# A two-block transformer kernel on one core: input norm reordered, rotations joined in pairs, norm boundaries and last quarter rearranged, two up projections 512 wide

## The chip, the cores and the metric

The kernel runs on one core of one Trainium2 chip. The metric is the device time of one execution in microseconds (us), as the median of several runs. The engines are named as in the profile: PE is TensorE's matmul side and PEld its weight loads, DVE is VectorE, ACT is ScalarE, POOL is GpSimd, and SP is SyncE, whose queue issues most DMAs.

## What is computed

The input has 256 tokens of width 1024. A first block puts 16 meta tokens in front and computes a convolution branch and a sparse attention branch, merged by gates, then an FFN with a short convolution. A second block of four steps follows (gated linear attention, FFN, block attention, FFN), each with a residual and a layer norm. All of it is fp32.

```python
h = rms_norm(stream, mix_norm_g[l])                 # stream: 16 meta tokens + x
u_conv, q, k, v, q_idx, k_idx, w_idx, gates = jnp.split(h @ w_in[l], split_at, axis=-1)
q = rope(q.reshape(bsz, seq_len, N_HEADS, HEAD_DIM), pos)
k = rope(k.reshape(bsz, seq_len, N_KV_HEADS, HEAD_DIM), pos)
q_idx = rope(...); k_idx = rope(...)
y_a = conformer_conv_branch(...)  # a*sigmoid(gate), 31-tap depthwise conv, layer norm, silu, @ pw_out
y_b = dsa_sparse_attention(...)   # keys chosen by index scores, softmax, @ w_o
g_a, g_b = jnp.split(jax.nn.sigmoid(gates), 2, axis=-1)
stream = stream + (g_a * y_a + g_b * y_b) @ w_merge_out[l]
h = rms_norm(stream, ffn_norm_g[l])
up = causal_depthwise_conv(h @ ffn_up[l], ffn_dw_w[l], ffn_dw_b[l])
a, b_ = jnp.split(up, 2, axis=-1)
stream = stream + (jax.nn.silu(a) * b_) @ ffn_down[l]
...
# second block, for the GLA mixer and then the MoBA mixer:
#   x = layer_norm_2(ALPHA * x + mixer(x));  x = layer_norm_2(ALPHA * x + swiglu_ffn(x))
# swiglu_ffn: gate, up = split(x @ w_gu); (silu(gate) * up) @ w_down
```

## The kernel before, in words

**Matmuls.** Every operand is split into a high and a low fp32r part, and a product is three matmuls: high by high, high by low, low by high. `mm_ws` (L175 to L177) keeps the weights stationary and streams the activations, transposed as hT, oT and so on (256 to 272 wide). `mm_xs` (L181 to L183) keeps the activations stationary and streams 512 columns of weights. Eight k steps of such triples make one projection tile (`proj_tile`). There are four PSUM buffers named ps_acc and four named ps_wk, each 512 wide.

**Weights.** They stream from DRAM in chunks of 2048 columns on SP's queue (wraw, three buffers). ACT makes the high part of a half chunk (whi, L134) and DVE the low one (wlo, L136), five halves ahead.

**The first block.** The input norm (from L283 on) transposes the raw x on PE, gets the row factors rw by `rsqrt` and `spread`, and forms hT in its two parts on ACT (L333) and DVE (L344). Then come the convolution's input (hp), keys, index heads, gates, eight query heads and the attention. `rope` rotates a head: two ACT copies swap the halves into sw, DVE multiplies by the tables twice and adds. Index scores are L474 and L477, softmax is L534 to L538, attention output oT has its low part made at L202.

**The convolution** of 31 taps is background work. Most taps are multiply-adds on DVE (L389, into yc). Some products are made on ACT (L406): one kind goes to a tile z with two buffers of its own tag, and DVE adds it to yc (L412); the other kind goes to zs, and a POOL DMA adds it into ysum, which DVE adds to yc at the end (L423). After that the layer norm of the convolution runs at high priority (L645 to L654 on DVE and PE's L648), and its result sT is needed for the projection by pw_out. While it runs, PE does the eight output projections of the attention (L175 to L177 from oT); DVE's L664 takes each out of its ps_acc buffer.

**Order.** A scheduler turns the program order into one queue for each engine: what is written earlier has priority, and each engine then works its queue strictly in order. At the norm boundaries and at the input norm the order is written out by hand: the strings in `ORDER` for the four layer norms name steps of `LayerNorm` (capital letters for the first 128 rows, small ones for the second: A add, S stats, G rsqrt, C center, F finish, L low part; g, x, t, k for other steps). `to_T` (L245) transposes a normed tile for the next projection.

**FFNs 2 and 3** (the SwiGLU ones): up projections in ps_wk, `evac2` (L936, L937) makes silu(a)·b, `split` its two parts rg_h and rg_l (L200, L202), and `mm_xs` the down projection into four ps_acc quarters, in groups of two hidden tiles; a ring keeps the last tiles of the FFN for the end. Then `norms` and the output.

Of the kernel before, what the change touches and what calls it, by code (L numbers as in the profile page):

```python
# [59 lines left out]
WARM = 9  # L60
FIRST = []
for _k in range(KT + 1):
# [22 lines left out]
def tile_hybrid(ctx: ExitStack, tc: tile.TileContext, x, meta, wts, misc, vec, cst, rows, gkw, ng, pos,  # L85
# [93 lines left out]
    def mm_xs(ps, xk, w, first, last):  # L179
        (wh, wl), (xh, xl) = w, xk  # L180
        PE.matmul(ps, xh, wh, start=first, stop=False)  # L181
        PE.matmul(ps, xh, wl, start=False, stop=False)  # L182
        PE.matmul(ps, xl, wh, start=False, stop=last)  # L183
# [38 lines left out]
    hT = (per.tile([P, KT, L], F32R, name="hT_h"), per.tile([P, KT, L], F32R, name="hT_l"))  # L222
# [18 lines left out]
    def to_T(src, xT, t, g, defer=False):  # L241
        pt = ps_wk().rearrange("p (a b) -> p a b", a=4)
        for a in range(4):
            k = 4 * g + a
            PE.transpose(pt[:, a, :], src[:, k * P:(k + 1) * P], ident)  # L245
# [35 lines left out]
    pj = ps_acc()  # L281
    for _ in range(WARM):
        PE.matmul(pj[:, :P], ones, ones, start=True, stop=True)  # L283
# [13 lines left out]
    with tc.high_priority(), tc.manual_schedule(engines={ENG.PE, ENG.DVE, ENG.Activation}):  # L297
        for k in range(KT):
            PE.transpose(pm[:, k * META:(k + 1) * META], mt[:, k * P:(k + 1) * P], ident[:META, :META])
        turn(0)  # L300
# [9 lines left out]
        A.activation(rw[:, :META], pr[:, :META], AF.Copy)  # L310
# [5 lines left out]
        for t in range(2):  # L316
            spread(rs[:, t:t + 1], META + t * P, P)
# [107 lines left out]
    def rope(o, ps, a, b, ti, parts=()):  # L425
        n = b - a
        sw = sc.tile([P, L], F32, name="sw", tag="s1", bufs=2)[:, :n]
        t1 = sc.tile([P, L], F32, name="t1", tag="s2", bufs=3)[:, :n]
# [21 lines left out]
    qi = []  # L450
    qi4 = mp.tile([P, 4, SEQ], F32, name="qi", tag="qi")
    for j in range(4):
        pq = ps_acc()
        proj_tile(pq[:, :SEQ], hT, META, L)
        q_ = qi4[:, j, :]
        rope(q_, pq[:, :SEQ], META, L, 2)
        qi.append(q_)
# [62 lines left out]
    qT = mp.tile([P, KT, NQ], F32, name="qT", tag="qT")  # L520
    for h in range(N_HEADS):
        pq = ps_acc()
        proj_tile(pq[:, :NQ], hT, T0, L)
        rope(qT[:, h, :], pq[:, :NQ], T0, L, 0)
# [6 lines left out]
    def soft(ps, b, n):  # L531
        l_ = sc.tile([P, L], F32, name="l_", tag="s2", bufs=3)[:, :n]
# [177 lines left out]
    def ffn(xT, n, pd, first, evac, ring, begun=None, then=None):  # L710
        f = 0
        while f < NF:
# [5 lines left out]
            for j in range(f, f + g):  # L718
# [4 lines left out]
                proj_tile(pa[:, :n], xT, 0, n, late=j == 0)  # L723
                proj_tile(pb[:, :n], xT, 0, n, late=j == 0)
# [38 lines left out]

    pd = [[ps_acc(), ps_acc()] for _ in range(2)]
# [7 lines left out]
    with tc.high_priority(), tc.manual_schedule(engines={ENG.DVE, ENG.Activation}):  # L772
        for t in range(2):
# [8 lines left out]
            for nn in range(2):  # L782
                s = slice(nn * 512, (nn + 1) * 512)
                V.scalar_tensor_tensor(x_[:, s], pd[t][nn], r, fg[:, s], op0=OP.mult, op1=OP.mult)
                lo.append(to_T(x_, hT, t, nn, defer=True))
# [9 lines left out]
    HV = [slice(nn * 512, (nn + 1) * 512) for nn in range(2)]  # L795

    class LayerNorm:
        def __init__(self, t, gi):
# [3 lines left out]
            self.bs = sc.tile([P, 2, 6], F32, name="bs", tag="bs", bufs=2)  # L802

        def add(self, nn):
# [3 lines left out]
        def stats(self, nn):  # L808
            V.bn_stats(self.bs[:, nn, :], self.y[:, HV[nn]])
# [11 lines left out]
        def finish(self, nn):  # L821
            s = HV[nn]
# [73 lines left out]
    def xs_late(ps, ws, t):  # L896
# [5 lines left out]
        for k, (wh, wl), c in at:  # L902
            PE.matmul(ps, hT[1][:, k, sl], wh[:, c], start=False, stop=k == KT - 1)  # L903

    def ffn_first(ring):
# [6 lines left out]
        def act(t):  # L912
            ps = first.ps[t]
            g_ = sc.tile([P, SEQ], F32, name="g_", tag="s2", bufs=3)
# [19 lines left out]
    def evac2(f, pa, pb):  # L934
        g_ = sc.tile([P, SEQ], F32, name="g_", tag="s2", bufs=3)
        A.activation(g_, pa[:, :SEQ], AF.Silu)  # L936
        V.tensor_mul(g_, g_, pb[:, :SEQ])  # L937
# [254 lines left out]
    ffn(hT, SEQ, pd, True, evac2, ring, begun)  # L1192
# [126 lines left out]
```

## Time and profile before

| what | us |
|---|---|
| runs | 1075.49, 1076.04, 1076.05 |
| median | 1076.04 |
| the profiled execution's own time | 1076.28 |
| its span, first to last instruction | 1074.5 |
| PE busy | 1054.8 (98%) |
| PEld busy | 954.5 (89%) |
| DVE busy | 739.5 (69%) |
| ACT busy | 601.0 (56%) |
| POOL busy | 44.1 (4%) |

All numbers taken from the trace are against the span. A matmul's duration in the trace holds a modelled end, so the cost of one is read from start to start, not from its duration. A row of the timeline is start, length, engine, line, operation, output and inputs, shapes, the number of instructions joined in it, and in brackets how long the engine was idle before it and what ended that.

### The profile page before, as it was taken

What the parts mean: (1) busy time and instruction counts of PE and PEld (TensorE: products, weight loads), DVE (VectorE), ACT (ScalarE), POOL (GpSimd) and SP (SyncE); (2) the same over time, 40 slices, a digit from 0 to 9 for tenths busy, and PEclk for the clock granted to TensorE, in tenths of its full rate; (3) what the DMA queues carried; (4) which work ended last, traced back from release to release, by engine and by line L of the source; (5) the groups of instructions that cost most, each with busy time, mean ns of one, the idle gap of its engine ahead of it and who ended that gap; (6) DMA issues with size and microseconds to landing.
All of it is one profiled execution on the core that took longest, in us unless ns stands there. A gap on an engine that the chain in (4) does not pass through costs nothing. (4 is left out here: it accounts for less than half of the span.)

```text
span 1074.5 us, 17515 instructions
## 1 busy us (share of the span) xinstructions
PE 1054.8 (98%) x6989; PEld 954.5 (89%) x6989; DVE 739.5 (69%) x1291; ACT 601.0 (56%) x1051; POOL 44.1 (4%) x52
## 2 busy tenths in 40 slices
PE   8999999999999999999999999999999999999997
PEld 8998998899899999977877999999888878999995
DVE  6899999995776767774577655556674766555555
ACT  6897698564555555567463444446256925444440
POOL 0131002100000000000000000000000000000000
PEclk8999999999999999999999999999999999999999
DMA  8886556564354555454453655557263436555541
GB/s 307 246 201 161 191 166 178 148 220 169 142 197 160 195 182 192 174 185 139 153 202 112 236 196 179 180 191 274 79 215 138 164 131 226 187 195 194 173 144 40
DMA packets 33333, 192.37 MB, mean 179 GB/s; under 512 B 3889, under 2 KB 7857, under 8 KB 12002
## 3 DMA queue, kind: packets, MB, share of 16 engines
q1 hardware_dynamic: 28002, 185.02, 49.7%
q0 software_dynamic: 5248, 6.23, 3.6%
q8 instruction: 55, 0.90, 0.3%
q14 instruction: 28, 0.23, 0.1%
HBM read 183.96 MB, written 1.05 MB: 172 GB/s over the span
## 5 line engine op out<-in xcount | busy, mean ns | idle before, releaser
L136 DVE TENSOR_TENSOR wlo<-wraw,whi 128x1024 fp32r<-128x1024 f32 x320 | 388.5, 1223 | 204.8 <-ACT whi L134 203.9
L134 ACT ACTIVATE whi<-wraw 128x1024 fp32r<-128x1024 f32 x322 | 337.3, 1058 | 302.0 <-PE ps_wk L176 117.7
L176 PE MATMUL ps_wk<-hT_l,whi 128*128 128x256 f32 (+1 forms) x976 | 274.9, 282 | 0.0
L177 PE MATMUL ps_wk<-hT_h,wlo 128*128 128x256 f32 (+1 forms) x976 | 274.6, 281 | 0.0
L175 PE MATMUL ps_wk<-hT_h,whi 128*128 128x256 f32 (+1 forms) x976 | 274.2, 281 | 0.0
L175 PEld LDWEIGHTS ps_wk<-hT_h,whi 128*128 128x128 f32 x976 | 184.4, 189 | 1.1
L176 PEld LDWEIGHTS ps_wk<-hT_l,whi 128*128 128x128 f32 x976 | 184.0, 189 | 1.4
L177 PEld LDWEIGHTS ps_wk<-hT_h,wlo 128*128 128x128 f32 x976 | 184.8, 189 | 0.4
L181 PE MATMUL ps_acc<-whi,rg_h 128*128 128x512 f32 x328 | 131.1, 400 | 0.0
L182 PE MATMUL ps_acc<-wlo,rg_h 128*128 128x512 f32 x328 | 129.6, 395 | 0.0
L183 PE MATMUL ps_acc<-whi,rg_l 128*128 128x512 f32 x328 | 127.1, 395 | 0.0
L175 PE MATMUL ps_acc<-hT_h,whi 128*128 128x258 f32 (+2 forms) x352 | 101.9, 290 | 0.0
L177 PE MATMUL ps_acc<-hT_h,wlo 128*128 128x258 f32 (+2 forms) x352 | 100.7, 286 | 0.0
L176 PE MATMUL ps_acc<-hT_l,whi 128*128 128x258 f32 (+2 forms) x352 | 100.5, 285 | 0.0
L183 PEld LDWEIGHTS ps_acc<-whi,rg_l 128*128 128x128 f32 x328 | 61.6, 188 | 14.7 <-DVE rg_l L202 0.2
L181 PEld LDWEIGHTS ps_acc<-whi,rg_h 128*128 128x128 f32 x328 | 61.6, 188 | 14.1 <-ACT rg_h L200 0.2
L182 PEld LDWEIGHTS ps_acc<-wlo,rg_h 128*128 128x128 f32 x328 | 61.7, 188 | 12.8
L181 PE MATMUL ps_acc<-whi,hT_h 128*128 128x512 f32 (+1 forms) x184 | 71.8, 390 | 0.0
L183 PE MATMUL ps_acc<-whi,hT_l 128*128 128x512 f32 (+1 forms) x184 | 70.8, 385 | 0.0
L182 PE MATMUL ps_acc<-wlo,hT_h 128*128 128x512 f32 (+1 forms) x184 | 70.6, 384 | 0.0
L175 PEld LDWEIGHTS ps_acc<-hT_h,whi 128*128 128x128 f32 x352 | 66.2, 188 | 0.3
L176 PEld LDWEIGHTS ps_acc<-hT_l,whi 128*128 128x128 f32 x352 | 66.3, 188 | 0.2
(950 smaller groups left out, 1561.7 us busy)
## 6 DMA issues: line engine op xcount, KB each, us to landing
wraw<-in_wts_dram SPq DMA_DIRECT2D x166, 1024.0 KB, 5.0
ysum<-zs POOLq DMA_DIRECT2D x10, 258.0 KB, 6.9
x<-in_x_dram SPq DMA_DIRECT2D x4, 512.0 KB, 3.8
lg<-in_rows_dram SPq DMA_DIRECT2D x4, 512.0 KB, 3.6
lb<-in_rows_dram SPq DMA_DIRECT2D x4, 512.0 KB, 5.4
wraw<-in_wts_dram SPq DMA_DIRECT2D x2, 512.0 KB, 6.5
out_dram<-x SPq DMA_DIRECT2D x4, 256.0 KB, 2.0
mraw<-in_misc_dram SPq DMA_DIRECT2D x1, 576.0 KB, 12.3
```

What stands on the lines that cost most here:

```text
L134: A.activation(hi, r, AF.Copy)
L136: V.tensor_sub(lo, r, hi.bitcast(F32))
L175: PE.matmul(ps, wh, xh, start=first, stop=False)
L176: PE.matmul(ps, wh, xl, start=False, stop=False)
L177: PE.matmul(ps, wl, xh, start=False, stop=last)
L181: PE.matmul(ps, xh, wh, start=first, stop=False)
L182: PE.matmul(ps, xh, wl, start=False, stop=False)
L183: PE.matmul(ps, xl, wh, start=False, stop=last)
```

## The change

1. **Input norm.** The first x tile is transposed after the meta tokens' row factor is spread; the two copies of rw go from ACT to DVE; the spread of the x rows' factors comes after the meta part of hT; five warm products on PE follow it.
2. **Rotations.** `rope_two` rotates two index heads (both in one ps_acc) or two query heads (the first six) in joined instructions. The swapped halves are in a tile sw2 with the tag z, that is in the two buffers of the convolution's z.
3. **Buffers.** Tag s2 (t1, l_, g_) has four buffers instead of three.
4. **Up projections of FFNs 2 and 3.** `proj_pair` streams the high and the low part of hT, which are now one tile, in one 512-wide matmul against the high weights, then the high part alone against the low weights. `evac2` adds the two halves of the result.
5. **Norm boundaries.** Manual dependencies (`BEHIND`) put the first transposes of each tile behind a certain matmul at the end of the first block; x and g change places in the first string of `ORDER`.
6. **Last quarter.** In the last FFN the last six hidden tiles of the last quarter go to two 256-wide ps_wk tiles; the last layer norm takes them in two pieces, with the sum of the residual and the rest (p1) ahead.

```diff
-WARM = 9
+WARM = (9, 5)
+BEHIND = (3, 2)
 ORDER = (
-    "A0 S0 A1 S1 G C0 C1 a0 F0 F1 s0 a1 L0 s1 L1 g x c0 c1 f0 f1 l0 l1 k x",
+    "A0 S0 A1 S1 G C0 C1 a0 F0 F1 s0 a1 L0 s1 L1 x g c0 c1 f0 f1 l0 l1 k x",
...
-    "A0 S0 A1 S1 G C0 C1 F0 F1 a0 s0 a1 s1 g c0 c1 f0 f1",
+    "p1 A0 S0 A1 S1 G C0 C1 F0 F1 a0 s0 a1 s1 a2 s2 g c0 c1 f0 f1 f2",
+    def proj_pair(ps):
+        w = next_half()
+        both = ps.rearrange("p (a b) -> p a b", a=2)
+        for k in range(KT):
+            wh, wl = cols(w, k * P, (k + 1) * P)
+            PE.matmul(both, wh, hT2[:, :, k, :SEQ], start=k == 0, stop=False)
+            PE.matmul(ps[:, :SEQ], wl, hT2[:, 0, k, :SEQ], start=False, stop=k == KT - 1)
...
-        turn(0)
...
-        A.activation(rw[:, :META], pr[:, :META], AF.Copy)
+        V.tensor_copy(rw[:, :META], pr[:, :META])
+        turn(0)
         turn(1)
...
-        for t in range(2):
-            spread(rs[:, t:t + 1], META + t * P, P)
...
+        for t in range(2):
+            spread(rs[:, t:t + 1], META + t * P, P)
+        for _ in range(WARM[1]):
+            PE.matmul(pz[:, :P], ones, ones, start=True, stop=True)
         later = []
-        A.activation(rw[:, META:], pr[:, META:], AF.Copy)
         emit_split(1, later)
+        V.tensor_copy(rw[:, META:], pr[:, META:])
...
+    def rope_two(o, ps, a, b, ti):
+        n = b - a
+        two = lambda i: tabs[:, i:i + 1, a:b].to_broadcast([P, 2, n])
+        sw = mp.tile([P, 2, NQ], F32, name="sw2", tag="z", bufs=2)[:, :, :n]
+        if len(ps) == 1:
+            both = ps[0].rearrange("p (a b) -> p a b", a=2)
+            A.activation(sw[0:64], both[64:128], AF.Copy)
+            A.activation(sw[64:128], both[0:64], AF.Copy)
+            V.tensor_mul(o, both, two(ti))
+        else:
+            for i, p in enumerate(ps):
+                A.activation(sw[0:64, i, :], p[64:128], AF.Copy)
+                A.activation(sw[64:128, i, :], p[0:64], AF.Copy)
+                V.tensor_mul(o[:, i, :], p, tabs[:, ti, a:b])
+        V.tensor_mul(sw, sw, two(ti + 1))
+        V.tensor_add(o, o, sw)
...
     for h in range(N_HEADS):
-        pq = ps_acc()
-        proj_tile(pq[:, :NQ], hT, T0, L)
-        rope(qT[:, h, :], pq[:, :NQ], T0, L, 0)
+        pqs.append(ps_acc()[:, :NQ])
+        proj_tile(pqs[-1], hT, T0, L)
+        if h >= N_HEADS - 2:
+            rope(qT[:, h, :], pqs[-1], T0, L, 0)
+        elif h % 2 == 1:
+            rope_two(qT[:, h - 1:h + 1, :], pqs[-2:], T0, L, 0)
...
+            if f + g == NF and ends:
+                order = order[:-g]
...
+            if f + g == NF and ends:
+                for a in range(0, 512, 256):
+                    ps = ps_wk()[:, :256]
+                    for i in range(g):
+                        mm_xs(ps, (acts[i][0][:, P:], acts[i][1][:, P:]), cols(ws[i], 512 + a, 768 + a),
+                              i == 0, i == g - 1)
+                    lasts.append(ps)
...
     def evac2(f, pa, pb):
-        g_ = sc.tile([P, SEQ], F32, name="g_", tag="s2", bufs=3)
-        A.activation(g_, pa[:, :SEQ], AF.Silu)
-        V.tensor_mul(g_, g_, pb[:, :SEQ])
+        g_, u_ = (sc.tile([P, SEQ], F32, name="g_", tag="s2", bufs=4) for _ in range(2))
+        A.activation(g_, pa[:, SEQ:], AF.Copy)
+        V.tensor_add(g_, g_, pa[:, :SEQ])
+        A.activation(g_, g_, AF.Silu)
+        A.activation(u_, pb[:, SEQ:], AF.Copy)
+        V.tensor_add(u_, u_, pb[:, :SEQ])
+        V.tensor_mul(g_, g_, u_)
         return g_
```

In the rows that follow the number behind a name tells tiles of one name apart. Lines are those of the changed kernel where rows are of the changed kernel: L406 there is L389 before (taps), L429 is L412 (z adds), L440 is L423 (final adds), L702 is L664, L686 is L648, L211 is L202, L137 is L136, L209 is L200, L1011 to L1016 are `evac2`.

DVE at the end of the convolution, before: the two splits of the last attention output, and the first output projection's gate product L664.

```order
L202 TENSOR_TENSOR oT_l_1518<-ps_wk_2286,oT_h_1517 128x4x128
L389 SCALAR_TENSOR_TENSOR yc_734<-hp_240,dwh_239,yc_734 128x243 x4
L389 SCALAR_TENSOR_TENSOR yc_734<-hp_240,dwh_239,yc_734 128x242
L202 TENSOR_TENSOR oT_l_1518<-ps_wk_2291,oT_h_1517 128x4x128
L389 SCALAR_TENSOR_TENSOR yc_734<-hp_240,dwh_239,yc_734 128x242
L423 TENSOR_TENSOR yc_734<-yc_734,ysum_2297 128x1032 x2
L136 TENSOR_TENSOR wlo_2698<-wraw_2101,whi_2697 128x1024
L645 TENSOR_TENSOR sqb_2618<-yc_734 128x516 x2
L664 SCALAR_TENSOR_TENSOR tg1_1520<-tg1_1520,ps_acc_2696 128x258
```

The same place after, from the second split on:

```order
L211 TENSOR_TENSOR oT_l_1490<-ps_wk_2263,oT_h_1489 128x4x128
L406 SCALAR_TENSOR_TENSOR yc_739<-hp_245,dwh_244,yc_739 128x258 x3
L429 TENSOR_TENSOR yc_739<-yc_739,z_2508 128x2x257
L406 SCALAR_TENSOR_TENSOR yc_739<-hp_245,dwh_244,yc_739 128x257 x2
L406 SCALAR_TENSOR_TENSOR yc_739<-hp_245,dwh_244,yc_739 128x256 x2
L406 SCALAR_TENSOR_TENSOR yc_739<-hp_245,dwh_244,yc_739 128x255 x4
L406 SCALAR_TENSOR_TENSOR yc_739<-hp_245,dwh_244,yc_739 128x254 x2
L406 SCALAR_TENSOR_TENSOR yc_739<-hp_245,dwh_244,yc_739 128x253 x2
L429 TENSOR_TENSOR yc_739<-yc_739,z_2530 128x2x253
L406 SCALAR_TENSOR_TENSOR yc_739<-hp_245,dwh_244,yc_739 128x252 x4
```

And after, the end of that run:

```order
L429 TENSOR_TENSOR yc_739<-yc_739,z_2568 128x2x245
L406 SCALAR_TENSOR_TENSOR yc_739<-hp_245,dwh_244,yc_739 128x245 x2
L406 SCALAR_TENSOR_TENSOR yc_739<-hp_245,dwh_244,yc_739 128x244 x2
L406 SCALAR_TENSOR_TENSOR yc_739<-hp_245,dwh_244,yc_739 128x243 x4
L406 SCALAR_TENSOR_TENSOR yc_739<-hp_245,dwh_244,yc_739 128x242 x2
L137 TENSOR_TENSOR wlo_2670<-wraw_2073,whi_2669 128x1024
L440 TENSOR_TENSOR yc_739<-yc_739,ysum_2269 128x1032
L702 SCALAR_TENSOR_TENSOR tg1_1492<-tg1_1492,ps_acc_2668 128x258
```

Where one tap stood behind the last split, 45 taps and five z adds stand there now (the rows between the two pieces go on in the same way).

PE at the convolution's layer norm, before: output projection 3 is in ps_acc_2790, and the sum over channels L648 stands ten matmuls into it.

```order
L175 MATMUL ps_acc_2790<-oT_h_1517,whi_2187 128x258
L176 MATMUL ps_acc_2790<-oT_l_1518,whi_2187 128x258
L177 MATMUL ps_acc_2790<-oT_h_1517,wlo_2188 128x258
L175 MATMUL ps_acc_2790<-oT_h_1517,whi_2187 128x258
L648 MATMUL ps_wk_2619<-sqb_2618,ones_77 128x258 x2
```

After, the last rows ahead of the same sum (L686):

```order
L176 MATMUL ps_acc_2792<-oT_h_1489,whi_2201 128x258
L177 MATMUL ps_acc_2792<-oT_l_1490,whi_2201 128x258
L178 MATMUL ps_acc_2792<-oT_h_1489,wlo_2202 128x258
L176 MATMUL ps_acc_2792<-oT_h_1489,whi_2201 128x258
L686 MATMUL ps_wk_2591<-sqb_2590,ones_77 128x258 x2
```

The sum has moved from output projection 3 to 13 matmuls into output projection 4 (ps_acc_2792), which is the fifth to ask for one of the four ps_acc buffers.

ACT in a group of FFN 2, before (L936 is the silu, L200 makes rg_h):

```order
L134 ACTIVATE whi_6852<-wraw_6762 128x1024
L936 ACTIVATE g__6880<-ps_wk_6820 128x256
L134 ACTIVATE whi_6887<-wraw_6762 128x1024
L200 ACTIVATE rg_h_6453<-g__6880 128x256
L134 ACTIVATE whi_6917<-wraw_6826 128x1024
```

After:

```order
L135 ACTIVATE whi_6794<-wraw_6712 128x1024
L1011 ACTIVATE g__6814<-ps_wk_6770 128x256
L1013 ACTIVATE g__6814<-g__6814 128x256
L1014 ACTIVATE g__6815<-ps_wk_6771 128x256
L135 ACTIVATE whi_6826<-wraw_6712 128x1024
L209 ACTIVATE rg_h_6425<-g__6814 128x256
```

Two copies out of PSUM are new, the second of them after the group's last up projection and ahead of a weight split.

More of the change, by code (lines that the diff above doesn't have):

```diff
@@ L182, in mm_xs @@
         PE.matmul(ps, xh, wl, start=False, stop=False)
-        PE.matmul(ps, xl, wh, start=False, stop=last)
+        return PE.matmul(ps, xl, wh, start=False, stop=last)
     def cols(w, a, b):
@@ L221, in tile_hybrid @@
     V.memset(ones, 1.0 / D)
-    hT = (per.tile([P, KT, L], F32R, name="hT_h"), per.tile([P, KT, L], F32R, name="hT_l"))
+    hT2 = per.tile([P, 2, KT, L], F32R, name="hT")
+    hT = (hT2[:, 0], hT2[:, 1])
     gl = [per.tile([P, KT, 16], F32R, name=f"gl{i}") for i in range(2)]
@@ L239, in row_bcast, with behind, to_T @@
         return t
-    def to_T(src, xT, t, g, defer=False):
+    def behind(turned, mark):
+        tc.add_manual_dep(turned.ins, mark.ins.name, LATER, reason="order")
+    def to_T(src, xT, t, g, defer=False, turned=None):
         pt = ps_wk().rearrange("p (a b) -> p a b", a=4)
@@ L279, in tile_hybrid @@
     nc.sync.dma_start(mraw, misc.rearrange("p (a b) -> p a b", a=KT))
-    pj = ps_acc()
-    for _ in range(WARM):
+    pj, pz = ps_acc(), ps_acc()
+    for _ in range(WARM[0]):
         PE.matmul(pj[:, :P], ones, ones, start=True, stop=True)
@@ L708, in tile_hybrid, with ffn @@
         go_on()
-    def ffn(xT, n, pd, first, evac, ring, begun=None, then=None):
+    def ffn(xT, n, pd, first, evac, ring, begun=None, then=None, ends=False):
         f = 0
@@ L722, in ffn @@
                 pa, pb = ps_wk(), ps_wk()
-                proj_tile(pa[:, :n], xT, 0, n, late=j == 0)
-                proj_tile(pb[:, :n], xT, 0, n, late=j == 0)
+                for ps in (pa, pb):
+                    if begun:
+                        proj_pair(ps)
+                    else:
+                        proj_tile(ps[:, :n], xT, 0, n, late=j == 0)
                 if begun and j == 2:
@@ L762, in evac1 @@
         return g_
+    marks, firsts = {}, []
     pd = [[ps_acc(), ps_acc()] for _ in range(2)]
@@ L784, in tile_hybrid @@
                 V.scalar_tensor_tensor(x_[:, s], pd[t][nn], r, fg[:, s], op0=OP.mult, op1=OP.mult)
-                lo.append(to_T(x_, hT, t, nn, defer=True))
+                turned = []
+                lo.append(to_T(x_, hT, t, nn, defer=True, turned=turned))
+                if nn == 0 and t == 0:
+                    behind(turned[0], marks[0])
+                elif nn == 0:
+                    firsts.append(turned[0])
             for f in lo:
@@ L801, in __init__, with add @@
             self.st = sc.tile([P, 8], F32, name="st8", tag="st8", bufs=3)
-            self.bs = sc.tile([P, 2, 6], F32, name="bs", tag="bs", bufs=2)
-        def add(self, nn):
+            self.parts = ENDS if (t, gi) == (1, 3) else HV
+            self.bs = sc.tile([P, 4, 6], F32, name="bs", tag="bs", bufs=2)[:, :2 * len(self.parts) - 2]
+        def add(self, nn, pre=False):
+            if self.parts is ENDS and nn and not pre:
+                s = ENDS[nn]
+                V.tensor_add(self.y[:, s], self.y[:, s], lasts[nn - 1])
+                return
             s = HV[nn]
@@ L808, in stats @@
         def stats(self, nn):
-            V.bn_stats(self.bs[:, nn, :], self.y[:, HV[nn]])
+            if self.parts is HV:
+                V.bn_stats(self.bs[:, nn, :], self.y[:, HV[nn]])
+                return
+            s = self.parts[nn]
+            for a in range(s.start, s.stop, 256):
+                V.bn_stats(self.bs[:, a // 256, :], self.y[:, a:a + 256])
         def center(self, nn):
@@ L853, in steps @@
                         go_on()
+                    elif op == "p1":
+                        ln[1].add(1, pre=True)
                     else:
@@ L902, in xs_late @@
         for k, (wh, wl), c in at:
-            PE.matmul(ps, hT[1][:, k, sl], wh[:, c], start=False, stop=k == KT - 1)
+            mm = PE.matmul(ps, hT[1][:, k, sl], wh[:, c], start=False, stop=k == KT - 1)
+            if k == BEHIND[1] and t == 0 and firsts:
+                behind(firsts.pop(), mm)
     def ffn_first(ring):
```

38 lines of the change are left out of this document (23 added, 15 removed).

## Prediction

> **What bounds the kernel now.** I read the page's busy shares first, then its forty slices.
>
> ```profile
> PE 1054.8 (98%) x6989; PEld 954.5 (89%) x6989; DVE 739.5 (69%) x1291; ACT 601.0 (56%) x1051; POOL 44.1 (4%) x52
> PE   8999999999999999999999999999999999999997
> DVE  6899999995776767774577655556674766555555
> ```
>
> TensorE is the bound, so time can come only from fewer or shorter matmuls, from the few microseconds in which PE stands, and from the ends. But VectorE is at nine tenths from the third to the ninth slice (54 to 242 us), where the background convolution runs. There it has little to give before PE waits. The waits of PE, and two windows around the end of the attention, say how near it is (a wait's numbers are us in total, times, longest):
>
> ```profile
> PE ps_acc L358 <- ACT hT_h L333: 2.7, 1, 2.7
> PE ps_wk L638 <- POOL rs L635: 1.9, 2, 1.4
> PE ps_wk L474 <- ACT r L477: 1.8, 2, 1.6
> PE ps_wk L245 <- DVE x L784: 1.1, 2, 0.6
> PE ps_wk L580 <- DVE q L578: 0.8, 1, 0.8
> PE ps_wk L648 <- DVE sqb L646: 0.4, 1, 0.4
> 130.00:196.00 66.00, 65.88 (x478) 58.62 (x479) 65.15 (x169) 57.47 (x162) 12.31 (x13) 1.00 0.64 170
> 196.00:222.00 26.00, 23.75 (x190) 22.77 (x190) 23.00 (x48) 15.58 (x28) 2.11 (x2) 1.00 0.48 154
> ```
>
> In the window rows the columns are length, then busy time of PE, PEld, DVE, ACT and POOL, the granted clock of PE, and the DMAs' share and GB/s. From 130 to 196 us DVE works 65.15 of 66 us: a tap that is late there stays late.
>
> **The convolution's tail, the term that decides.** The timeline of VectorE at the end of the convolution:
>
> ```profile
> 183.04 2.80 DVE L389 SCALAR_TENSOR_TENSOR yc<-hp,dwh,yc 128x250 f32<-128x250 f32 x7
> 185.75 1.23 DVE L136 TENSOR_TENSOR wlo<-wraw,whi 128x1024 fp32r<-128x1024 f32 x1
> 187.88 0.44 DVE L534 CUSTOM_DVE_ANT_0 l__2269<-ps_wk,bias 128x272 f32<-128x272 f32 x1
> 189.36 0.16 DVE L538 RECIPROCAL st<-st 128x1 f32<-128x1 f32 x1
> 190.96 0.67 DVE L412 TENSOR_TENSOR yc<-yc,z 128x490 f32<-128x490 f32 x1
> 191.54 1.62 DVE L389 SCALAR_TENSOR_TENSOR yc<-hp,dwh,yc 128x245 f32<-128x245 f32 x4
> 195.69 0.69 DVE L202 TENSOR_TENSOR oT_l<-ps_wk,oT_h 128x512 fp32r<-128x512 f32 x1
> 196.30 0.46 DVE L389 SCALAR_TENSOR_TENSOR yc<-hp,dwh,yc 128x242 f32<-128x242 f32 x1
> 198.59 1.23 DVE L423 TENSOR_TENSOR yc<-yc,ysum 128x1032 f32<-128x1032 f32 x1 [0.69 <-DMA ysum<-zs]
> 199.75 1.22 DVE L136 TENSOR_TENSOR wlo<-wraw,whi 128x1024 fp32r<-128x1024 f32 x1
> 202.09 0.42 DVE L664 SCALAR_TENSOR_TENSOR tg<-tg,ps_acc 128x258 f32<-128x258 f32 x1
> ```
>
> Seven taps from 183.04 to 185.75 are 0.387 us each, start to start; a z add is 0.58 (190.96 to 191.54). The last softmax reciprocal stands at 189.36. After it VectorE has 9 taps, a z add and the two splits of the attention output left until 196.30, then one tap and the final adds; the convolution ends at 199.75, 10.3 us after the reciprocal is done (189.43).
>
> The change gives the swapped halves of the joined rotations (sw2) the two buffers of tag z. They are allocated in the program ahead of the convolution's z tiles, which then get their turn only when the rotations are done. VectorE's new order shows the result. After the last reciprocal come 3+6+4+1 taps, two z adds and the two splits: 14×0.387 + 2×0.58 + 2×0.61 = 7.8 us. Behind the last split stand 45 taps (17.4), 5 z adds (2.9), a weight split (1.14) and one final add (1.16): 22.6 us. Together 30.4 against 10.3 us, so the convolution ends 20.1 us later, counted from the reciprocal. That reciprocal I hold in place, since VectorE takes the last scores (187.88) as PE has just made them: PE's chain sets it, and PE is busy 65.88 of 66 us there.
>
> Does PE have other work for that long? No. From the last attention product on it has 75 matmuls of the output projections 0 to 3 and then output 4. That needs a ps_acc buffer, which the first gate product frees (L664 before, L702 after), and this stands behind all 45 taps. The timeline of PE has 30 such matmuls here, in 3.45 us from the first start to the last, of which these are the ends:
>
> ```profile
> 196.06 0.28 PE L176 MATMUL ps_acc<-oT_l,whi 128*128 128x258 f32 x1
> 199.51 0.28 PE L177 MATMUL ps_acc<-oT_h,wlo 128*128 128x258 f32 x1
> ```
>
> 0.119 us each, so 75 are 8.9 us against the 22.6 us behind the split. PE stands for some 14 us, then again for L686 and through the layer norm that follows. Before, PE already waited at L648 in this place: VectorE sets the pace, nothing covers the delay, and 20.1 us go on the path. The ends of this term: 20.1 if the reciprocal stays; 9.8 if VectorE never idled from 126 to the end (its row has 65.15 of 66 us busy; the moved order has 83.6 us of work from the first query product on, 126 + 83.6 = 209.6 against 199.75). I take the upper one, since VectorE cannot run ahead of the scores that PE makes. The lower one already holds the earlier waits below.
>
> **What comes back earlier.** At the second attention bias the order leaves VectorE 58.1 us of convolution to do (each tap and add at the prices above) against 43.2 before: it has 15 us less until then. So L474's 1.8 us and L580's 0.8 should mostly go. Both ends: 0 and -2.6; I take -2.0, as the pairs also make the first rotation of each wait for its second head. The joined rotations themselves: a 512-wide pass takes 0.61 on VectorE (195.69 to 196.30), two 256-wide ones at most 2×0.42 (202.09's 258-wide row); some ten such pairs save it 2 us at most, and PE nothing. The fourth s2 buffer, the reordered reloads on SP and the earlier memsets on POOL I cost at nothing: PE waits for none of these queues in the list above, and x is reloaded long before use.
>
> **After the standstill, the clock.** It is the third column from the end of these rows, at the start of the kernel:
>
> ```profile
> 13.00:16.00 3.00, 2.87 (x10) 2.44 (x11) 2.83 (x6) 2.85 (x6) 0.00 (x0) 0.50 1.02 421
> 16.00:19.50 3.50, 3.50 (x18) 3.50 (x17) 3.50 (x6) 2.15 (x4) 0.00 (x0) 0.50 0.64 263
> ```
>
> After 2.7 us without work the granted clock is 0.50 for 6.5 us. After 14 us of standing the same would cost 3.2 us, but the chain of the layer norm lets PE wait 1.4 at L638 and as much again at L686, so I add 0.5 (ends 0 and 3.2). The Trainium skill ("TensorE: Matmul & The Clock Gate", What's actually happening) says that the clock halves after an idle window of about 3.4 us and is whole again after as much sustained work; here 2.7 us were enough to halve it and 6.5 us were needed. By that rule the loss would be 1.7 us, all of it inside those waits, and the term 0.
>
> **Input norm.** PE's 2.7 us at L358 end when ACT has the first hT_h, which follows VectorE's h.
>
> ```profile
> 10.33 0.29 DVE L318 TENSOR_TENSOR hm<-ps_acc,rw 128x128 f32<-128x128 f32 x1 [2.40 <-PE ps_acc L290]
> 11.60 1.29 DVE L329 TENSOR_TENSOR h<-ps_wk,rw 128x512 f32<-128x512 f32 x2
> 12.96 0.99 PE L358 MATMUL ps_acc<-hT_h,whi 128*128 128x272 f32 x2 [2.73 <-ACT hT_h L333]
> ```
>
> The meta part (10.33 to 11.60) now runs before the second spread, which takes most of 1.2 us out of the path, and the copy of rw that moves from ACT to VectorE (128x256, 0.42) gives 0.4 back: h starts 0.7 us earlier. The five warm products fill PE's gap, so the clock may stay whole; but from 13 to 19.5 us VectorE is busy nearly all the time (2.83 of 3.00, 3.50 of 3.50), and PE soon waits for its lower halves. I take -1.0, ends +0.4 (the warm products run past the first hT_h) and -2.7.
>
> **Up projections 2 and 3.** 640 times two 256-wide products become one 512-wide (2 FFNs × 20 columns × 2 × 8). Pure stretches of both kinds, PE first:
>
> ```profile
> 902.87:914.06 11.19, 11.19 (x51) 9.02 (x49) 5.66 (x6) 4.54 (x5) 0.00 (x0) 1.00 0.50 163
> 914.06:925.41 11.35, 11.35 (x97) 11.35 (x96) 5.66 (x6) 5.09 (x7) 0.00 (x0) 1.00 0.57 199
> 902.75 0.28 PE L177 MATMUL ps_wk<-hT_h,wlo 128*128 128x256 f32 x1
> 906.12 0.40 PE L183 MATMUL ps_acc<-whi,rg_l 128*128 128x512 f32 x1
> 903.13 0.42 DVE L937 TENSOR_TENSOR g__9586<-g__9586,ps_wk 128x256 f32<-128x256 f32 x1 [0.64 <-PE ps_wk L177]
> 903.97 0.40 ACT L200 ACTIVATE rg_h<-g__9586 128x256 fp32r<-128x256 f32 x1
> 905.24 0.42 DVE L202 TENSOR_TENSOR rg_l<-g__9586,rg_h 128x256 fp32r<-128x256 f32 x1
> ```
>
> 48 starts of 512-wide matmuls fill the first (233.1 ns each), 96 of 256-wide the second (118.2; the rows' counts also hold matmuls cut by the edge). 2×118.2 − 233.1 = 3.3 ns, ×640 = -2.1 us. The Trainium skill (same page, Wait — 56ns, not 53.3ns?) gives each warm matmul a fixed 2.5 ns, by which this would be -1.6 us. The 640 weight loads that go lie beside matmuls. The price is the evacuation: a copy on ACT and an add on VectorE are new between the last product (902.75) and rg_l. Before, rg_l is ready at 905.66, and its first reader starts at 906.12: 0.46 us to spare. The copy and the add (0.4 each) put ACT's weight split, behind which the lower split waits, 0.5 later: rg_l comes at about 906.2. I put 0.08 us on each of 18 groups, +1.5 (ends 0, and 0.8 × 18 = 14 as below). Net -0.6.
>
> **Norm boundaries and tail.**
>
> ```profile
> 458.55 0.63 PE L245 MATMUL ps_wk<-cs,x 128*128 128x128 f32 x4 [0.64 <-DVE x L784]
> 469.98 0.63 PE L245 MATMUL ps_wk<-cs,x 128*128 128x128 f32 x4 [0.44 <-DVE x L784]
> 1066.80 0.69 DVE L806 SCALAR_TENSOR_TENSOR y<-x,ps_acc 128x512 f32<-128x512 f32 x1 [2.58 <-PE ps_acc L183]
> 1067.53 0.69 DVE L809 BATCH_NORM_STATS2 bs<-y 128x6 f32<-128x512 f32 x1
> ```
>
> Three 512-wide matmuls (0.7 us) now stand before each of the two groups of transposes, which covers the 0.64 and 0.44; with half of a similar wait at the first layer norm -1.4 (ends 0 and -1.9). At the end the last quarter is finished in two 256-wide pieces: the last add and the statistics shrink from 0.69 to about 0.42 each (the 128x256 rows), -0.54; 36 matmuls of 118.2 for 18 of 233.1 cost 0.06, and the extra output DMA shortens the last transfer a little: -0.6 (ends 0 and -1.0).
>
> **Sum**, against the profiled execution (span 1074.5, time 1076.28, 0.24 above the median of 1076.04): +20.1 − 2.0 + 0.5 − 1.0 − 0.6 − 1.4 − 0.6 = +15.0, so 1091.3 there and **1091 us** as a median.
>
> **Rivals.**
> - *All of it shows* (the forecast), 1086 to 1096: for it speaks that VectorE works its queue in order and PE waited at this very place before. Chance 0.66.
> - *Half of it shows*: VectorE does its late taps while it would wait for PE, the term is 9.8 net of the earlier waits. 1076.0 + 9.8 + 0.5 − 1.0 − 0.6 − 1.4 − 0.6 = 1083; down to 1077 if the softmaxes also come earlier. Against it: the scores come from PE. Chance 0.16, of which 0.03 within 0.2% of before.
> - *The tail of the convolution is covered* (the other side, and that the change does only what its parts say): the first gate product must come within 8.9 us of the last attention product, that is VectorE must be at least 14 us further along its queue than I count. Then only the gains stay: 1076.0 − 2.0 − 1.0 − 2.1 − 1.4 − 0.6 = 1069, or 1072 with the evacuation's price. For it: VectorE has spare time after 242 us and now some before 130. Chance 0.13.
> - *The FFN's evacuation shows too*: if copy and add lie wholly in the path, 18 groups lose 0.8 us each, 14 us on top: 1105. Chance 0.05; against it, 0.46 us to spare and both engines near half idle in these stretches (5.66 and 4.54 of 11.19 us).
>
> The measurement tells 0.2%, about 2.2 us, from no change. The range takes the forecast's 1086 to 1096 and the upper part of the second case, from 1080 on: about 0.8. Faster 0.13, same 0.03, slower 0.84.
>
> **What would show it.** In the changed profile: a wait of PE of 10 us or more near 195 to 215 us on the first output-4 matmul, released by L702, and a run of L406 taps on VectorE behind the last split; L474's and L580's waits gone; clock 0.5 after the stand; 640 matmuls fewer and the FFN's stretches shorter by about 0.03 us per column half; L258's waits gone; the last statistics at 0.42. I am wrong if VectorE idles long before the last reciprocal yet PE does not stand behind L702, or if PE's waits on rg_l grow past 2 us.

## The result: 1088.15 us against 1076.05, and the profile after

The changed kernel takes 1088.15 us (median of 4 runs, 1087.60 to 1088.63); the kernel before takes 1076.05 in the runs beside it. The ratio is 1.0109 with a 95% interval of 1.0097 to 1.0122: slower by 12 us. The profiled execution has a span of 1086.8 us against 1074.5, so 12.3 us are to be found.

The page of the changed kernel, busy shares and slices:

```profile
PE 1054.3 (97%) x6377; PEld 925.1 (85%) x6377; DVE 775.1 (71%) x1366; ACT 626.0 (58%) x1125; POOL 43.6 (4%) x52
PE   8999999499999999999999999999999999999997
DVE  7779999997577676865566756568665667565676
PEclk9999999799999999999999999999999999999999
```

One digit tells most of it: PE is busy four tenths in the eighth slice (190 to 217 us) where it had nine, and its clock is lower there. Four of PE's waits, the longest first (us in total, times, longest):

```profile
PE ps_acc L176 <- DVE tg L702: 17.4, 3, 16.2
PE ps_wk L618 <- DVE q L616: 1.4, 1, 1.4
PE ps_acc L375 <- DVE hT L361: 1.0, 1, 1.0
PE ps_wk L676 <- POOL rs L673: 0.5, 1, 0.5
```

One wait of 16.2 us is new, on the first matmul of output projection 4, released by L702, the first gate product. L474's wait (now L508) and those at the norm boundaries (L245, now L258) are gone from the list; the query product's (L580, now L618) has stayed and grown. VectorE's timeline at the place, with PE's row behind it:

```profile
184.69 0.15 DVE L576 RECIPROCAL st<-st 128x1 f32<-128x1 f32 x1
192.13 0.68 DVE L211 TENSOR_TENSOR oT_l<-ps_wk,oT_h 128x512 fp32r<-128x512 f32 x1
194.53 4.82 DVE L406 SCALAR_TENSOR_TENSOR yc<-hp,dwh,yc 128x257 f32<-128x257 f32 x12
202.02 4.74 DVE L406 SCALAR_TENSOR_TENSOR yc<-hp,dwh,yc 128x251 f32<-128x251 f32 x12
209.39 3.90 DVE L406 SCALAR_TENSOR_TENSOR yc<-hp,dwh,yc 128x245 f32<-128x245 f32 x10
214.36 1.22 DVE L440 TENSOR_TENSOR yc<-yc,ysum 128x1032 f32<-128x1032 f32 x1
215.50 0.41 DVE L702 SCALAR_TENSOR_TENSOR tg<-tg,ps_acc 128x258 f32<-128x258 f32 x1
215.96 0.58 PE L176 MATMUL ps_acc<-oT_h,whi 128*128 128x258 f32 x1 [16.21 <-DVE tg L702]
```

Behind the last split (192.13) VectorE does nothing but taps and z adds without a gap until 213. From the last reciprocal to the end of the convolution it is 215.50 − 184.76 = 30.7 us.

Where the convolution fell behind stands much earlier. Its z adds, before (L412) and after (L429), each row with the first and the last start:

```profile
L412 DVE TENSOR_TENSOR yc<-yc,z x22: 646/682/695, 40.8 to 191.0; 128x516 f32<-128x516 f32 x9, 128x502 f32<-128x502 f32 x2, 128x494 f32<-128x494 f32 x2, 128x510 f32<-128x510 f32 x1
L429 DVE TENSOR_TENSOR yc<-yc,z x22: 652/680/693, 115.4 to 208.8; 128x516 f32<-128x516 f32 x9, 128x502 f32<-128x502 f32 x2, 128x494 f32<-128x494 f32 x2, 128x510 f32<-128x510 f32 x1
```

The first z add comes at 115.4 us, when the joined query heads are being rotated (their copies on ACT start at 100.9 and end at 116.8); before, it came at 40.8. By 130 us VectorE has done 38 of its 140 taps, where it had done 55. The windows after, to be read as in the prediction:

```profile
68.00:130.00 62.00, 60.57 (x493) 59.54 (x492) 56.52 (x130) 41.33 (x76) 1.05 (x2) 1.00 0.41 141
130.00:196.00 66.00, 66.00 (x481) 59.18 (x481) 60.86 (x151) 64.55 (x187) 17.96 (x18) 1.00 0.71 169
```

VectorE is busy 56.52 and 60.86 us there, where it was busy 60.91 and 65.15: it had time to spare while the taps were held up. ACT, which makes the z products, is busy 64.55 of 66 us in the second window (57.47 before); whether it holds VectorE back there is not shown.

The shift of PE against the kernel before, read at the start of the same matmul in both traces, gives the ledger:

| place | before | after | shift |
|---|---|---|---|
| 101st projection matmul of the first block | 29.03 | 26.37 | -2.7 |
| first query product | 130.02 | 125.10 | -4.9 |
| last attention product | 194.43 | 190.13 | -4.3 |
| first sum of the convolution's layer norm (L648, now L686) | 203.17 | 218.92 | +15.8 |
| first FFN, first matmul | 274.74 | 288.74 | +14.0 |
| first FFN, 60 matmuls on | 282.05 | 297.55 | +15.5 |
| GLA mixer (the gate product) | 481.90 | 496.56 | +14.7 |
| MoBA mixer | 826.34 | 839.92 | +13.6 |
| last matmul | 1066.37 | 1079.29 | +12.9 |
| end of the span | 1074.5 | 1086.8 | +12.3 |

### The profile page after: what moved, and what is told of

Read it like the earlier page. It is cut to its first block, busy times and chain, and to the rows that moved or that the text cites. A ratio compares the mean times of both kernels' runs of the same rounds, so it can differ in the third digit from the quotient of the medians.

```text
span 1086.8 us, 16403 instructions
## 1 busy us (share of the span) xinstructions
PE 1054.3 (97%) x6377; PEld 925.1 (85%) x6377; DVE 775.1 (71%) x1366; ACT 626.0 (58%) x1125; POOL 43.6 (4%) x52
## 5 line engine op out<-in xcount | busy, mean ns | idle before, releaser
L137 DVE TENSOR_TENSOR wlo<-wraw,whi 128x1024 fp32r<-128x1024 f32 x320 | 388.6, 1223 | 179.8 <-ACT whi L135 176.5
L205 PE MATMUL ps_wk<-hT,whi 128*128 128x512 f32 x640 | 224.5, 393 | 0.0
L206 PE MATMUL ps_wk<-hT,wlo 128*128 128x256 f32 x640 | 179.5, 280 | 0.0
L205 PEld LDWEIGHTS ps_wk<-hT,whi 128*128 128x128 f32 x640 | 120.1, 188 | 27.4
L206 PEld LDWEIGHTS ps_wk<-hT,wlo 128*128 128x128 f32 x640 | 120.2, 188 | 0.7
L176 PE MATMUL ps_acc<-hT,whi 128*128 128x258 f32 (+2 forms) x352 | 102.1, 290 | 0.0
L178 PE MATMUL ps_acc<-hT,wlo 128*128 128x258 f32 (+2 forms) x352 | 100.7, 286 | 0.0
L177 PE MATMUL ps_acc<-hT,whi 128*128 128x258 f32 (+2 forms) x352 | 100.6, 286 | 0.0
L177 PE MATMUL ps_wk<-hT,whi 128*128 128x258 f32 x336 | 94.9, 282 | 0.0
L178 PE MATMUL ps_wk<-hT,wlo 128*128 128x258 f32 x336 | 94.7, 282 | 0.0
L176 PE MATMUL ps_wk<-hT,whi 128*128 128x258 f32 x336 | 94.7, 282 | 0.0
L182 PE MATMUL ps_acc<-whi,hT 128*128 128x512 f32 (+1 forms) x184 | 71.7, 390 | 0.0
L184 PE MATMUL ps_acc<-whi,hT 128*128 128x512 f32 (+1 forms) x184 | 70.8, 385 | 0.0
L183 PE MATMUL ps_acc<-wlo,hT 128*128 128x512 f32 (+1 forms) x184 | 70.7, 384 | 0.0
## 6 DMA issues: line engine op xcount, KB each, us to landing
mraw<-in_misc_dram SPq DMA_DIRECT2D x1, 576.0 KB, 12.3
```

What stands on the lines that cost most here:

```text
L137: V.tensor_sub(lo, r, hi.bitcast(F32))
L176: PE.matmul(ps, wh, xh, start=first, stop=False)
L177: PE.matmul(ps, wh, xl, start=False, stop=False)
L178: PE.matmul(ps, wl, xh, start=False, stop=last)
L184: return PE.matmul(ps, xl, wh, start=False, stop=last)
L205: PE.matmul(both, wh, hT2[:, :, k, :SEQ], start=k == 0, stop=False)
```

## The experiments

All but the fourth and the last change the new kernel; that one and the last add one part to the kernel before.

**The swapped halves in other buffers.**

```diff
-        sw = mp.tile([P, 2, NQ], F32, name="sw2", tag="z", bufs=2)[:, :, :n]
+        sw = mp.tile([P, 2, NQ], F32, name="sw2", tag=tag)[:, :, :n]   # tag: "qT" index heads, "qi" query heads
```

> The changed kernel with one edit: the swapped halves of the joined rotations are in tiles of tags qT (index heads) and qi (query heads), one buffer each, instead of in the two buffers of tag z. Theory A (the convolution's z tiles have to wait for the rotations, its taps move behind the attention, PE stands for L702): the order has no tap behind the last split, the stand of 16.2 us goes, and the other gains stay: 1088.15 - 16.2 - 1 to 2 = 1069 to 1073 us. Rival B (joining two heads itself delays the work, whatever the buffers are): PE still stands 10 us or more before output projection 4, 1084 us or more.

Measured: 1069.03 us, ratio to before 0.9940 (0.9925 to 0.9955). In VectorE's timeline the convolution ends at 196.8, before PE asks:

```profile
193.92 0.69 DVE L211 TENSOR_TENSOR oT_l<-ps_wk,oT_h 128x512 fp32r<-128x512 f32 x1
195.64 1.23 DVE L440 TENSOR_TENSOR yc<-yc,ysum 128x1032 f32<-128x1032 f32 x1 [1.02 <-DMA ysum<-zs]
199.14 0.41 DVE L702 SCALAR_TENSOR_TENSOR tg<-tg,ps_acc 128x258 f32<-128x258 f32 x1
```

and PE's longest waits are

```profile
PE ps_wk L508 <- ACT r L511: 1.9, 1, 1.9
PE ps_wk L618 <- DVE q L616: 0.8, 1, 0.8
PE ps_wk L686 <- DVE sqb L684: 0.7, 1, 0.7
```

The rotations are still joined, and 19 us are gone. So the two shared buffers are the cause, not the joining. The wait of the index scores is back (L508, 1.9), and VectorE is nearly full there again (61.45 of the 62 us from 68 to 130).

**Every head rotated alone.**

```diff
-        if j % 2 == 1:
-            rope_two(qi4[:, j - 1:j + 1, :], [pq], META, L, 2)
+        rope(qi4[:, j, :], pq[:, j % 2 * SEQ:(j % 2 + 1) * SEQ], META, L, 2)
...
-        if h >= N_HEADS - 2:
+        if True:
```

> The changed kernel with every head rotated alone as before (no rope_two, no sw2); all else as changed. Theory A: 1069 to 1073 us, within 2 us of the kernel that joins the rotations in other buffers, since the joined passes save VectorE about 2 us and PE nothing. If joining is worth something by itself, this one is slower than the other by 2 us or more; if joining costs, it is faster by as much.

Measured: 1068.47 us, ratio 0.9932 (0.9917 to 0.9946). Between the two the intervals overlap: joining the rotations is worth nothing that can be measured.

**sw2 in tag z for the index heads alone** (the query heads' in qi):

```diff
-            rope_two(qi4[:, j - 1:j + 1, :], [pq], META, L, 2, "qT")
+            rope_two(qi4[:, j - 1:j + 1, :], [pq], META, L, 2, "z")
```

> The changed kernel with sw2 in tag z for the index heads alone; the query heads' is in tag qi. Its order has 37 taps and 4 z adds behind the last split (19.1 us at the prices of the prediction) where the changed kernel has 45 and 5 (22.9). Theory A in its sharp form (what counts is the work that the order puts behind the last split): the stand is 3.8 us shorter, 12.4 us, and the time about 1084 us (1082 to 1087). Rival D (the z tiles are only held up until the rotation that holds the buffer is done): the index heads are rotated by 95 us, 100 us before the convolution's end, and nothing is lost: 1069 to 1073 us.

Measured: 1083.86 us, ratio 1.0076 (1.0061 to 1.0091), and in PE's timeline

```profile
211.86 0.58 PE L176 MATMUL ps_acc<-oT_h,whi 128*128 128x258 f32 x1 [11.48 <-DVE tg L702]
```

The stand is 4.7 us shorter for an order that has 3.8 us less behind the split, and the time 4.3. The stand follows the work behind the split, to within a microsecond. Rival D is out: two index pairs that are rotated by 95 us are enough. The first z add comes at 80.1 us here, between the 40.8 of the kernel before and the 115.4 of the changed one, and by 130 us VectorE has done 43 taps, where those two have 55 and 38. From 68 to 130 us it is busy 57.11 of 62 us, and the taps that were not done then stand behind the split.

**The joined rotations alone, on the kernel before.**

```diff
+    def rope_two(o, ps, a, b, ti): ...            # as in the change, sw2 in tag z
-        rope(q_, pq[:, :SEQ], META, L, 2)
+            rope_two(qi4[:, j - 1:j + 1, :], [pq], META, L, 2)
```

> The kernel before with the joined rotations alone (sw2 in tag z). Its order has 45 taps and 5 z adds behind the last split, as the changed kernel has. Theory A: VectorE runs ahead by some 2 to 3 us until the query heads, then PE stands 15 to 17 us before output projection 4: 1076 + 16 = 1092 us (1088 to 1095). Rival C (the delay comes only together with the other parts, say the fourth s2 buffer or the new order of the input norm): within 3 us of 1076.

Measured: 1092.18 us, ratio 1.0152 (1.0135 to 1.0169), with the same stand:

```profile
217.84 0.58 PE L175 MATMUL ps_acc<-oT_h,whi 128*128 128x258 f32 x1 [16.22 <-DVE tg L685]
```

One part alone makes the whole loss, and the others together gain.

**The up projections.** The next kernels rotate every head alone, so that the stand does not cover the rest; this kernel was run beside them once more:

> The changed kernel with every head rotated alone, once more, as the kernel that the next three are compared with: 1068.5 us, as in its first run (within 0.7).

It took 1069.99 us (1067.98 to 1071.04), 1.5 more than the first time and outside the 0.7 that were expected. The profiled execution, the longest of the six, shows a part of why: at two places (from 73.2 and from 271.1 us) the clock is halved for 3.4 us where the first run of the same kernel has 1.00 (below). Differences of a microsecond are therefore read at the places of the trace rather than from the medians.

The products with the lower half, last:

```diff
+                if begun and f + g < NF and i == g - 1:
+                    PE.matmul(pd[t][nn], xh, wh, start=False, stop=False)
+                    PE.matmul(pd[t][nn], xh, wl, start=False, stop=False)
+                    held.append((pd[t][nn], xl, wh, ...))
+                    continue
...
+            for ps, xl, wh, end in held:
+                PE.matmul(ps, xl, wh, start=False, stop=end)
```

> Heads rotated alone, and in FFNs 2 and 3 the down projection of the last tile of each group runs its eight products with rg_h first and its four with rg_l last, which gives rg_l 1.4 us more cover. Theory E (the new evacuation shows as the wait for rg_l, which the trace has at 3.9 us in 13 waits of 0.3 on PEld): these waits go, and of the 2.1 us that the wide products save the 1.1 us come back that are missing: 1067.4 us (1066.8 to 1068.0). Rival F (the missing part is not that wait: the wide product with its two pieces of hT is slower than counted): no change, 1068.5.

And the up projections as before:

```diff
-                    if begun:
-                        proj_pair(ps)
-                    else:
+                    if True:
                         proj_tile(ps[:, :n], xT, 0, n, late=j == 0)
```

> Heads rotated alone, and the up projections of FFNs 2 and 3 in three 256-wide products with the old evac2 (the s2 tag keeps its four buffers). The up projections are worth 1.05 us net by the shift between the two traces (14.64 to 14.0 us is the norm boundary's; FFN 2 0.4, FFN 3 0.65): 1069.5 us (1069.0 to 1070.2), with the waits for rg_l at 0.2 us. If they were worth the full 2.1: 1070.6; if nothing: 1068.5.

Measured: 1066.51 us with the lower half last, 1072.13 with the old up projections, 1069.99 between them; the first is 0.3 us under its expected range, the second 1.9 above. PEld's waits for rg_l in the changed kernel, and then with the lower half last (with the old up projections the row has 0.2 us in 1 wait as well):

```profile
PEld ps_acc L184 <- DVE rg_l L211: 4.1, 13, 0.5
```

```profile
PEld ps_acc L184 <- DVE rg_l L211: 0.2, 1, 0.2
```

Summed from start to start over FFNs 2 and 3, the 1920 products of the up projections take 227.2 us in the old form, and the 1280 of the new form 223.7 (the same with the lower half last). The down projection of a group of two tiles takes 5.60 us with the old evacuation, 5.74 with the new one, and 5.60 again with the lower half last; there are 12 such groups, and the larger groups lose nothing. So the wide products are worth 3.5 us, the wait for rg_l takes 1.6 of it, and putting the four products last gives that back. Theory E holds, with both sizes larger than expected, and rival F is out: within the up projections a 512-wide product takes 231.0 ns from start to start, less than the 233.1 that was counted.

**The norm boundaries as before.**

```diff
-        tc.add_manual_dep(turned.ins, mark.ins.name, LATER, reason="order")
+        pass
-    "A0 S0 A1 S1 G C0 C1 a0 F0 F1 s0 a1 L0 s1 L1 x g c0 c1 f0 f1 l0 l1 k x",
+    "A0 S0 A1 S1 G C0 C1 a0 F0 F1 s0 a1 L0 s1 L1 g x c0 c1 f0 f1 l0 l1 k x",
```

> Heads rotated alone, and the norm boundaries as before: the manual dependencies do nothing, and x and g stand in the old order in the first string of ORDER. By the shifts between the two traces (0.9 at the end of the first block, 0.7 at the first layer norm) this costs 1.6 us: 1070.1 us (1069.5 to 1070.6), with PE's waits at the first transposes of each tile back at 0.6 and 0.4. The rival, that these shifts came from something else there: 1068.5 with the waits back, covered later.

Measured: 1069.77 us, which by the medians is no difference from 1069.99. By the shifts against the kernel before, the stretch from the first FFN to the GLA mixer gains 0.9 us in the first run of the kernel with the boundaries (-4.4 to -5.3) and nothing here (-4.8 to -4.8); the next stretch, up to the start of FFN 2, gains 0.2 in that run (0.5 in the second run of the same kernel) and nothing here. PE's waits at the first transposes are back, with 0.64, 0.42 and 0.39 us. The boundaries are worth 1.2 to 1.4 us in the trace. The medians don't show it; the profiled execution of the reference has two halved stretches and the one of this kernel has none before its end, and what the other executions had is not in a trace.

**Input norm and tail.** The reference of these runs, the kernel with the lower half last:

> Heads rotated alone and the four products with rg_l last, once more, as the kernel that the next two are compared with: 1066.5 us (1065.8 to 1067.5).

It took 1067.49 us; ratio to before 0.9922 (0.9909 to 0.9936), 0.9913 (0.9899 to 0.9927) in its first run. Without the five warm products (`WARM = (9, 0)`):

> The same without the five warm products of the input norm (WARM = (9, 0)). Theory H (they keep PE's clock whole): the granted clock falls to 0.5 between about 12 and 18 us as in the kernel before, the first projections run at half pitch, and the time rises by 1.5 us (0.5 to 3). Rival G (VectorE makes the lower halves too slowly for PE to use a whole clock there): the clock falls and the time stays, within 0.4 us.

Measured: 1069.64 us. The windows from 13 to 19.5 us, first without them, then with them; the granted clock is the third number from the end:

```profile
13.00:16.00 3.00, 2.77 (x12) 2.77 (x13) 2.87 (x5) 1.78 (x5) 0.00 (x0) 0.50 1.02 417
16.00:19.50 3.50, 3.50 (x28) 3.50 (x28) 3.50 (x7) 3.23 (x5) 0.00 (x0) 0.94 0.91 323
```

```profile
13.00:16.00 3.00, 2.40 (x17) 2.19 (x17) 2.87 (x5) 1.72 (x5) 0.00 (x0) 1.00 1.03 420
16.00:19.50 3.50, 2.88 (x23) 2.88 (x24) 3.50 (x7) 3.29 (x5) 0.00 (x0) 1.00 0.99 343
```

They do keep the clock whole there (it is whole at this place in all eleven traces with them, and falls to half at 13.0 to 13.6 us in the three without), but the 101st projection matmul starts at 26.95 without and 26.79 with them: 0.16 us. VectorE (2.87 and 3.50 of the window) sets the pace, as rival G says. The time does not follow G, though: it rises by 2.1 us, which is in theory H's range. In the profiled execution the rest of it comes from a wait and a halved clock between 72 and 80 us (0.81 and 0.77 there). All five executions have a mean clock of 0.995, where the four of the reference have 0.997 or 0.998, so it is not one stray execution; how the missing products bring it about is open.

The tail as before (`ends=True` left out, the old last string of `ORDER`):

> Heads rotated alone, rg_l last, and the last quarter and the last layer norm as before (no 256-wide ends, no p1). The stretch from the start of the last matmul to the end of the span was 8.1 us before and 7.5 us after: +0.6 us here (0.3 to 0.9), 1067.1 us.

Measured: 1066.63 us, not slower than 1067.49. In the trace the stretch from the last matmul on is 8.1 us here and 7.5 there, as expected; but from the end of the MoBA mixer's products to the last matmul this kernel gains 1.7 us against the kernel before and the other 1.45, so the 256-wide ends cost 0.2 on the way. The other 0.8 us are from the start: the first projection starts at 11.04 here and 11.82 there, which differs by as much between two runs of one kernel (11.12 and 11.82). The tail is worth 0.4 us, below what the medians tell.

The input norm alone, on the kernel before (the input norm's part of the diff, nothing else):

> The kernel before with the reordered input norm alone. The first projection starts 1.1 to 1.9 us earlier at a whole clock, as in every kernel that has this part. If PE is bound from there to the index scores, the time falls by 1.6 us: 1074.4 us (1073.8 to 1075). Rival: VectorE is full until the index scores (convolution at its place), PE waits there for as much longer, and the time stays at 1075.5 to 1076.2.

Measured: 1073.83 us, ratio 0.9985 (0.9976 to 0.9994). The 101st projection matmul starts at 26.12 instead of 29.03. By the median the theory holds, with a gain of 2.1 us. The profiled execution is one of the longer ones (1075.20): by the first query product the gain has turned into +1.2, with longer waits of the index scores (1.5 and 1.9 us) and the clock at 0.50 between 88 and 92 us, and by the first FFN it is -1.2 again.

## Why the prediction was right, step by step

*The convolution's tail.* Right in place and size: +20.1 us were forecast from the reciprocal, and the shift goes from -4.3 to +15.8, 20.1 us, with 30.7 us from the reciprocal instead of 30.4. The half rival (9.8) and the covered one are out. PE's chain does set the last scores: PE is busy 66.00 of the 66 us from 130 to 196, and VectorE waits 1.6 us there for scores (L572 on L591), though taps are still left. With the shared buffers taken away the kernel takes 1069.03, where the covered rival had 1069; that is partly luck, as its -2.0 for earlier waits does not come (L508 waits 1.9 us there) and its input norm gives 2.0 instead of 1.0.

*Earlier waits.* -2.0 was forecast and -1.6 came (from -2.7 to -4.3), but not as told: the index scores' wait went, and the query product's stayed at 1.4 us.

*Input norm.* The term was mis-sized: -1.0 forecast, -2.7 measured in these two executions. The start came 1.6 us earlier (11.40 against 12.96) where 0.7 were counted: the spread of the x rows starts at 9.19 instead of 9.85, which the sum left out, and h at 10.12 instead of 11.60. VectorE's pace ate nothing of it, since its backlog began that much earlier too. The other 1.1 us, between the first projection and the 101st, are not the change's. That stretch takes 14.97 us in the changed kernel and 16.07 in the kernel before, but 14.96 in the kernel before with the joined rotations alone, which has the old input norm. VectorE's instructions follow each other at the same distances in these two; what differs is the clock. The windows of the one with the joined rotations:

```profile
13.00:16.00 3.00, 2.58 (x9) 2.05 (x10) 2.78 (x7) 3.00 (x7) 0.00 (x0) 0.61 1.02 419
16.00:19.50 3.50, 3.50 (x24) 3.30 (x24) 3.50 (x6) 2.01 (x5) 0.00 (x0) 0.85 0.68 279
```

The kernel before has 0.50 in both, with 18 matmuls in the second window instead of 24. So a halved clock of 3.4 us costs nothing here (15.06 in the kernel without warm products), and the 6.8 us that the profiled execution of the kernel before had cost it 1.1.

*Clock after the stand.* The clock did fall, to half until about 221 us, in the windows from 216 on:

```profile
199.50:216.00 16.50, 0.29 (x4) 0.07 (x2) 16.50 (x38) 5.74 (x13) 4.76 (x4) 0.62 0.66 113
216.00:218.00 2.00, 2.00 (x9) 2.00 (x10) 2.00 (x3) 0.00 (x0) 0.00 (x0) 0.50 1.04 414
218.00:220.00 2.00, 2.00 (x9) 1.73 (x8) 2.00 (x4) 0.00 (x0) 0.00 (x0) 0.50 0.79 315
220.00:222.00 2.00, 2.00 (x14) 1.87 (x13) 1.38 (x5) 0.60 (x2) 0.00 (x0) 0.83 0.39 53
```

Some five us at half, where the row at the kernel's start had 6.5. It made the first sum last 1.5 us instead of 0.8, and VectorE waited 0.6 for it. More than that came back, however: by the first FFN the shift has shrunk to 14.0, 1.8 us less. PE does 27 more products of the output projections ahead of the sum than before (13 into projection 4 instead of ten into projection 3), at 0.119 us each 3.2 us that no longer stand behind it, and the wait of 1.4 us at L638 is gone (the 0.5 of L676 in the list is that of the FFN's norm, 0.54 in both traces). The forecast +0.5 was thus 2.3 too high here; but 1.5 us came at another place, below. That much of the two errors cancels is luck.

*Up projections.* -0.6 forecast, about -2 measured (-1.4 in the one execution of the changed kernel). The gross gain was too small, 2.1 against 3.5. The 118.2 ns hold (118.3 over both FFNs), but the 233.1 ns for a 512-wide product were taken from the down projections, and in the new up projections it takes 231.0: 2×118.3 − 231.0 = 5.6 ns, times 640 is 3.6 us. The wait was 1.5 against 1.6, by luck: 18 groups at 0.08 us were counted, and 12 groups lose 0.14 each.

*Norm boundaries and tail.* -1.4 forecast, -1.2 to -1.4 by the experiment; -0.6 forecast for the tail, -0.6 at the end but 0.2 lost just ahead, where 0.06 was counted.

Measured less forecast in the executions compared: -1.7 (input norm, 1.1 of it the clock of the kernel before), +0.4 (earlier waits), -2.3 (chain after the stand), +1.5 (clock in the first FFN), +0.1 (boundaries), -0.8 (up projections), +0.2 (tail): -2.6, of the 2.7 by which +15.0 lies above the measured +12.3.

## What to carry to other kernels

A buffer tag is a place in a queue: a tile that is written earlier in the program, in a tag with two buffers, delayed every later tile of that tag here, and with it background work that has nothing to do with it. Where an engine works its queue in order, count what the new order puts between the last input of a critical step and that step; here that count times the trace's prices gave the loss within a microsecond, and moving the tile to a tag that is idle at the time turned 12 us lost into 7 won. The best of these kernels also puts the products that need the latest operand last in a group (1066.5 and 1067.5 us in two sets of runs).

## What the runs showed of the hardware

The granted clock can be halved for 3.4 us after a short thin stretch of PE, in one execution and not in another of the same kernel. The changed kernel has it at the start of the first FFN (windows of 1 us):

```profile
288.00:289.00 1.00, 0.45 (x4) 0.26 (x3) 1.00 (x4) 0.73 (x2) 0.00 (x0) 0.97 0.00 0
289.00:290.00 1.00, 1.00 (x6) 1.00 (x6) 1.00 (x4) 1.00 (x4) 0.00 (x0) 0.50 0.00 0
292.00:293.00 1.00, 1.00 (x9) 1.00 (x9) 1.00 (x5) 1.00 (x2) 0.00 (x0) 0.82 0.00 0
```

There 1.5 us are lost, behind two waits of 0.54 and 0.55 us (L676 and L193) that the kernel before has too, with the same lengths, at a whole clock. The kernel with every head rotated alone, in its two profiled executions at that place (first the first run):

```profile
272.00:276.00 4.00, 4.00 (x35) 4.00 (x34) 4.00 (x11) 2.97 (x5) 0.00 (x0) 1.00 0.00 0
```

```profile
272.00:276.00 4.00, 4.00 (x25) 4.00 (x25) 4.00 (x12) 4.00 (x8) 0.00 (x0) 0.68 0.00 0
```

35 matmuls against 25 in the same 4 us. The two executions ran on different chips; but on one chip, too, the mean clock of the six executions of the second set goes from 0.995 to 0.999. So a microsecond or two between two kernels can be the clock's and not the change's, and the 1.5 us above are not counted to the change. The Trainium skill ("TensorE: Matmul & The Clock Gate", What's actually happening) has the activity watched in a free-running window of about 3.4 us; a halving that comes and goes between executions with the same gaps, and lasts about that long, agrees with it. So do the clock records of the traces: away from the end of the kernels every halved stretch lasts 3.41 us or a multiple of it (6.83 at the start of the kernel before, 13.65 in the stand of the kernel with the index heads alone in tag z, 17.07 in that of the changed kernel). That the clock falls after less than 3.4 us without work (2.73 us at the start of the kernel before) agrees only if the window need not be wholly idle.
